# Two decoder layers on one core: the MLP up product of six chunks in eight with the weights as the standing operand

## Chip, cores and metric

One core of one Trainium2 chip runs the whole program in one launch. The metric is the device time of that core in microseconds (us), the median of several executions; less is better. TensorE does the matrix products (a load of the standing 128x128 operand, LDWEIGHTS, and then a matmul that streams the other operand through it), VectorE (DVE) and ScalarE (ACT) do elementwise work and empty the accumulators (PSUM, 8 banks of 512 float32 columns), GpSimd (POOL) does a few small steps, and SyncE (SP) issues the transfers (DMA).

## What is computed

Two layers over 256 tokens of width 1024. Layer 0 mixes tokens by block attention, layer 1 by differential attention; the attention code is not touched, apart from the layout of its operands. After it comes the MLP that the change is about, and each half of a layer is closed by a LayerNorm and scaled and shifted by modulation vectors made from a conditioning vector:

```python
def sq_relu_mlp(h, w_up, w_down):          # w_up 1024x4096, w_down 4096x1024
    return jnp.square(jax.nn.relu(h @ w_up)) @ w_down
...
for i in range(DEPTH):                     # DEPTH = 2
    h = x * (1.0 + scale1) + shift1
    y = moba_attention(...) if i % 2 == 0 else diff_attention(...)
    x = layer_norm(DEEPNORM_ALPHA * x + (1.0 + gate1) * y, ...)
    h = x * (1.0 + scale2) + shift2
    y = sq_relu_mlp(h, mlp_w_up[i], mlp_w_down[i])
    x = layer_norm(DEEPNORM_ALPHA * x + (1.0 + gate2) * y, ...)
```

All is float32. The modulation vectors are `silu(c) @ ada_w + ada_b`, twelve vectors of 1024.

## The kernel before, in words

**Three passes.** A float32 product is made of three matmuls: each operand is split into a rounded part `hi` (type float32r) and the remainder `lo`, and `hi*hi + hi*lo + lo*hi` is summed in PSUM (`mm3`, L165 to L168). A weight arrives by DMA in a raw tile of 128x2048 (three buffers); ACT makes `hi` of a piece of 128x1024 (L129), DVE makes `lo` (L130); there are eight buffers of each. A chunk of 512 columns of `w_up` (`load_cols`) or of 512 rows of `w_down` (`load_rows`) is four such pieces.

**Tokens in two blocks.** The 256 tokens are two blocks of 128, b = 0 and 1. The modulated input of a block is transposed so that the width lies on the partitions, and split: tiles `hTh` and `hTl`, of 128 x 4 x 128, two pairs for each block, four buffers each. These 128x128 slices are the standing operand; the weights stream.

**MLP.** The 4096 inner columns are eight chunks of 512 (`NJ`). Step U (`step_up`) makes the up product of a block and a chunk: 8 slices of the width times 3 passes are 24 matmuls that stream 512 weight columns each into one bank `mm`; ACT applies relu and square (L642, L643) into a tile `nat`, with tokens on the partitions. The down product needs the inner columns on the partitions, so step X (`step_up_T`) transposes the tile by four matmuls against an identity (L650) into a bank `tp`, and ACT and DVE split it into `sTh` and `sTl` (L653, L654). Step D (`step_down`) then runs 24 matmuls of 512 columns (L183): 4 slices, 3 passes, 2 halves of the output. The accumulators of D are two banks `ac` for block 0 and two banks `sc` for block 1, open over all eight chunks.

**Boundaries.** Step B (`boundary`) prepares the vectors of the LayerNorm that closes a half layer: it calls `need`, which traces what is still missing of the gate, scale and shift vectors, and broadcasts the gate (L114, L116). Step C (`close`) does the LayerNorm of a block (L275, L278, L288, ..., L294) and `modulate`, which transposes the result (L307) and fills `hTh` and `hTl` (L311, L314, L315) for the next half layer.

**Modulation vectors as filler.** Each vector is eight rows (`ada_rows`, L214 the DMA of 512 KB, L215 a multiply and sum on DVE) and a closing step, in a queue `filler`. A step `f3` in the program takes three from the queue. The residual of a closed block (L320, L321) is put at the head of the same queue.

**Order.** The string `PROGRAM` lists the steps of each layer; their order in it is the order in which they are traced, and this is the priority by which the framework's scheduler fills each engine's queue, at compile time: where the first in line can't yet run by its model of time, one behind it is taken. Each engine and SP's DMA queue then runs its list strictly in order. The tile framework sets the waits, from the tiles and slices that instructions read and write.

Of the kernel before, what the change touches and what calls it, by code (L numbers as in the profile page):

```python
# [16 lines left out]
F32 = mybir.dt.float32  # L17
# [31 lines left out]
    O11 C10 U00 U01 X00 U10 U11 X01 f1 X10 D00 f1 X11 U02 f2 U12 D10 f1 X02 f1 D01 f1 X12 D11 f3 U03 U13  # L49
    f2 X03 D02 f1 X13 f1 U04 f3 U14 D12 f2 X04 D03 f1 X14 D13 U05 f2 U15 f2 X05 D04 f1 X15 D14 f1 U06 f2  # L50
    U16 f2 X06 D05 f1 X16 D15 f1 U07 f2 U17 f2 X07 D06 X17 f1 D07 f1 B1 C01 D16 D17 C11
# [4 lines left out]
    C10 U00 U01 X00 U10 X01 U11 X10 D00 f1 X11 D10 f1 U02 f3 U12 f2 X02 D01 f1 X12 D11 f1 U03 f2 U13 f2  # L56
    X03 D02 f1 X13 D12 f1 U04 f2 U14 f2 X04 D03 f1 X14 D13 f1 U05 f3 U15 f2 X05 D04 f1 X15 D14 f1 U06 f2
    U16 f2 X06 D05 f2 X16 D15 U07 f2 U17 f2 X07 D06 X17 D07 f1 B1 C01 E C11
# [16 lines left out]
def tile_trunk(ctx: ExitStack, tc: tile.TileContext, x, c, moba_w_in, moba_w_out, diff_w_in, diff_w_out,  # L75
# [60 lines left out]
    def load_cols(w, segs):  # L136
        """[1024, 512] columns, as segments (start, width) -> list of KC (hi, lo) [128, 512] operands."""
# [15 lines left out]
    def load_rows(w, r0):  # L153
        """[512, 1024] row segment -> list of 4 (hi, lo) [128, 1024] operands."""
# [20 lines left out]
    def dense2(dsts, lhs, rows, start, stop):  # L175
        """rows: (hi, lo) of [128, 1024]; dsts: the two column halves."""
# [33 lines left out]
    def ada_rows(l, v, j, dst, tag, bufs):  # L210
        """Chunk j of modulation vector v of layer l as a column: sum_k w[k, n] silu(c)[k] + ada_b[n]."""
# [25 lines left out]
    def affine_cols(l, first, prev):  # L237
        """A = g (1 + scale), B = b (1 + scale) + shift for the LayerNorm `prev` feeding this sub-layer."""
# [11 lines left out]
    def pair_tile(tag, bufs):  # L250
        return (ap_.tile([P, 4, P], F32R, tag=tag + "h", name=tag + "h", bufs=bufs),
                ap_.tile([P, 4, P], F32R, tag=tag + "l", name=tag + "l", bufs=bufs))

    def as_ops(pairs):
        return [(h[:, k, :], l[:, k, :]) for h, l in pairs for k in range(4)]

# [9 lines left out]
    def layer_norm(b, accs, gate, parts=None):  # L266
        """z = alpha x + gate y and its statistics; normalised unless `parts` gives the columns as they come."""
# [32 lines left out]
    def modulate(z, A, B):  # L300
        pairs = []
        for h in range(2):
            hi, lo = pair_tile("hT", 4)
# [12 lines left out]
            pairs.append((hi, lo))  # L316
        return pairs
# [7 lines left out]
    # Head pairs are taken in four groups of two; a group's q and k columns form one product.  # L325
# [39 lines left out]
    def softmax(b, sc, sums, scol_i):  # L365
        """sc: [128, 128 or 256] scores in PSUM -> exp(scale (s - max)), row sums in sums[:, scol_i]."""
# [10 lines left out]
    def probs_T(b, mats):  # L377
        """Transposes of [128, n] tiles; returns per matrix the list of [128 keys, 128 queries] operands."""
# [14 lines left out]
    def scores(b, g):  # L393
        """{(pair, component): [128, 128 (b + 1)] PSUM view}; the two row halves use separate banks."""
# [63 lines left out]
    def attend_finish(kind, b, g, on):  # L458
# [3 lines left out]
        if g % 2 == 0:  # L462
            oT[b, g // 2] = pair_tile("sT", 4)
        hi, lo = (t[:, (g % 2) * 2:(g % 2) * 2 + 2, :] for t in oT[b, g // 2])
# [10 lines left out]
    hT0 = [[pair_tile("hT", 4) for _ in range(2)] for _ in range(2)]  # L475
    # v, then q and k of groups 0 and 1
    kacc = [[psum(t) for t in ("mm", "sc", "ac")] for _ in range(2)]

    def first_operand(j):
        """Modulated operand chunk j of both blocks, and the weight rows that meet it."""  # L480
# [23 lines left out]
        for b in range(2):  # L504
            hi, lo = hT0[b][j // 4]
            act.copy(out=hi[:, j % 4, :], in_=full[:, b * P:(b + 1) * P])
            vec.tensor_tensor(out=lo[:, j % 4, :], in0=full[:, b * P:(b + 1) * P], in1=hi[:, j % 4, :], op=ALU.subtract)
# [4 lines left out]
    def first_products(j, ws):  # L512
        for b in range(2):
            hi, lo = hT0[b][j // 4]
# [90 lines left out]
    def step_v(st, b, g2):  # L605
# [20 lines left out]
    def step_out(st, b, g2):  # L626
# [3 lines left out]
        out_proj(acc, g2, b, rows)  # L630

    def step_close(st, b, i):
        l = st["l"]
        st["x", b] = close(l, i, b, st["oacc" if i == 0 else "dacc", l, b], st["bd"])

    def step_up(st, b, j):
# [3 lines left out]
        dense(ps, as_ops(st["x", b]), w)  # L640
# [5 lines left out]
    def step_up_T(st, b, j):  # L646
# [4 lines left out]
        hi, lo = pair_tile("sT", 4)  # L651
# [84 lines left out]
```

## Time and profile before

| | us |
|---|---|
| median of 3 runs | 662.51 |
| lowest and highest run | 658.27, 663.25 |
| profiled execution, from the first to the last instruction (span) | 663.8 |
| MLP of layer 0, about | 165 to 335 |
| attention of layer 1, about | 360 to 460 |
| MLP of layer 1, about | 480 to 643 |

For the profiled execution the page gives its span and no other time. Times in the profile count from the first instruction. Busy time of PE (matmul) and of PEld (LDWEIGHTS) overlap each other, and a matmul's recorded length is longer than its distance to the next, since matmuls are pipelined: the pace is read from the starts. A row of the view of the groups gives line, engine, operation, result and operand names, shapes and count, then busy time and mean length in ns, and last the idle time before and what ended it.

### The profile page before, as it was taken

To read this page: it belongs to the slowest core of one execution; us is meant where nothing else is said; L and a number is where in the kernel's file an instruction comes from. 1 tells how busy PE (TensorE), PEld (TensorE's weight loads), DVE (VectorE), ACT (ScalarE), POOL (GpSimd) and SP (SyncE) were. 2 spreads that over 40 slices of the span, in tenths; PEclk is the share of its full clock that TensorE was granted. 3 is DMA by queue.
4 is the path that set the end of the run, shared out by engine and by line. 5 is a ranking of instruction groups with operands and counts; after the bars stand their busy time and mean duration, and the time that the engine had idled before them with its cause. 6 is when DMAs were issued, how large, how long until landed. Compare 5 with 4: busy or idle time off the path is not lost. (4 is left out here: it accounts for less than half of the span.)

```text
span 663.8 us, 8530 instructions
## 1 busy us (share of the span) xinstructions
PE 630.3 (95%) x3044; PEld 506.1 (76%) x3044; DVE 484.9 (73%) x855; ACT 365.4 (55%) x651; POOL 22.2 (3%) x37
## 2 busy tenths in 40 slices
PE   4999999999999999999969999989999999999994
PEld 3767878877888888888757887767788888888883
DVE  4798899789968677776689978886974535454446
ACT  3457766457654455555255676765774555354520
POOL 0000000000000000000000010021100000000001
PEclk9999999999999999999979999999999999999998
DMA  8987998876789979888953877661565564636401
GB/s 294 408 313 264 315 315 289 295 239 205 268 258 337 325 252 340 318 292 289 358 195 128 297 252 262 236 222 37 182 228 189 169 210 152 227 129 197 183 1 63
DMA packets 65941, 158.23 MB, mean 238 GB/s; under 512 B 4042, under 2 KB 21099, under 8 KB 65899
## 3 DMA queue, kind: packets, MB, share of 16 engines
q1 hardware_dynamic: 65898, 157.68, 68.0%
q8 instruction: 24, 0.39, 0.2%
q14 instruction: 19, 0.15, 0.1%
HBM read 156.62 MB, written 1.05 MB: 238 GB/s over the span
## 5 line engine op out<-in xcount | busy, mean ns | idle before, releaser
L130 DVE TENSOR_TENSOR lo<-raw,hi 128x1024 fp32r<-128x1024 f32 x196 | 231.2, 1198 | 62.7 <-ACT hi L129 60.5
L129 ACT CAST hi<-raw 128x1024 fp32r<-128x1024 f32 x196 | 200.8, 1037 | 65.4 <-PE sc L183 24.4
L166 PE MATMUL mm<-hi,hTh 128*128 128x512 f32 x416 | 167.4, 403 | 5.1 <-ACT hi L129 2.5
L168 PE MATMUL mm<-hi,hTl 128*128 128x512 f32 x416 | 166.6, 400 | 0.0
L167 PE MATMUL mm<-lo,hTh 128*128 128x512 f32 x416 | 165.8, 399 | 0.1
L215 DVE CUSTOM_DVE_ANT_0 aw<-aw,sbc,tabT 128x1024 f32<-128x1024 f32 x96 | 121.8, 1282 | 43.4 <-DMA aw<-in_ada_w_dram 43.2
L166 PEld LDWEIGHTS mm<-hi,hTh 128*128 128x128 f32 x416 | 78.5, 189 | 24.4 <-ACT hi L129 2.9
L168 PEld LDWEIGHTS mm<-hi,hTl 128*128 128x128 f32 x416 | 78.6, 189 | 18.3 <-DVE hTl L315 0.4
L167 PEld LDWEIGHTS mm<-lo,hTh 128*128 128x128 f32 x416 | 78.6, 189 | 18.1 <-DVE lo L130 0.3
L642 ACT ACTIVATE nat<-mm 128x512 f32<-128x512 f32 x32 | 19.1, 597 | 63.6 <-PE mm L168 63.5
L183 PE MATMUL ac<-hi,sTh 128*128 128x512 f32 x160 | 52.2, 405 | 0.0
L183 PE MATMUL ac<-lo,sTh 128*128 128x512 f32 x160 | 50.8, 395 | 0.0
L183 PE MATMUL ac<-hi,sTl 128*128 128x512 f32 x160 | 50.7, 395 | 0.1
L183 PE MATMUL sc<-hi,sTh 128*128 128x512 f32 x144 | 46.7, 405 | 0.0
L183 PE MATMUL sc<-hi,sTl 128*128 128x512 f32 x144 | 45.5, 396 | 0.0
L183 PE MATMUL sc<-lo,sTh 128*128 128x512 f32 x144 | 45.3, 396 | 0.0
L653 ACT CAST sTh<-tp 128x512 fp32r<-128x512 f32 x32 | 18.7, 584 | 46.2 <-PE tp L650 46.2
L654 DVE TENSOR_TENSOR sTl<-tp,sTh 128x512 fp32r<-128x512 f32 x32 | 22.0, 690 | 24.5 <-ACT sTh L653 24.5
L183 PEld LDWEIGHTS ac<-hi,sTl 128*128 128x128 f32 x160 | 29.8, 188 | 6.7 <-DVE sTl L654 0.5
L183 PEld LDWEIGHTS ac<-lo,sTh 128*128 128x128 f32 x160 | 30.0, 188 | 6.3
L373 ACT ACTIVATE p<-sc,mx 128x128 f32<-128x128 f32 (+1 forms) x64 | 26.6, 421 | 12.1 <-DVE mx L370 10.7
L183 PEld LDWEIGHTS ac<-hi,sTh 128*128 128x128 f32 x160 | 28.7, 189 | 4.8
(137 smaller groups left out, 673.3 us busy)
## 6 DMA issues: line engine op xcount, KB each, us to landing
aw<-in_ada_w_dram SPq DMA_DIRECT2D x96, 512.0 KB, 5.4
raw<-in_mlp_w_up_dram SPq DMA_DIRECT2D x32, 1024.0 KB, 7.1
raw<-in_mlp_w_down_dram SPq DMA_DIRECT2D x32, 1024.0 KB, 5.7
raw<-in_diff_w_in_dram SPq DMA_DIRECT2D x16, 512.0 KB, 4.5
raw<-in_moba_w_in_dram SPq DMA_DIRECT2D x24, 256.0 KB, 5.6
raw<-in_moba_w_in_dram SPq DMA_DIRECT2D x8, 512.0 KB, 5.4
raw<-in_moba_w_out_dram SPq DMA_DIRECT2D x4, 1024.0 KB, 7.9
raw<-in_diff_w_in_dram SPq DMA_DIRECT2D x4, 1024.0 KB
```

Of the source, the lines that this page charges most:

```text
L129: act.copy(out=hi[:, :n], in_=raw_ap)
L130: vec.tensor_tensor(out=lo[:, :n], in0=raw_ap, in1=hi[:, :n], op=ALU.subtract)
L166: pe.matmul(dst, lhsT=xh, rhs=wh, start=start, stop=False)
L167: pe.matmul(dst, lhsT=xh, rhs=wl, start=False, stop=False)
L168: pe.matmul(dst, lhsT=xl, rhs=wh, start=False, stop=stop)
L183: pe.matmul(dsts[h], lhsT=a, rhs=w[:, h * 512:(h + 1) * 512], start=start and k == 0 and i == 0, stop=stop and k == n - 1 and i == 2)
L215: vec.tensor_tensor_reduce(out=aw, in0=aw, in1=sbc, scale=1.0, scalar=adab_cols(l, v)[:, j:j + 1], op0=ALU.mult, op1=ALU.add, accum_out=dst)
L373: act.activation(out=pt[:, :n], in_=sc, func=AF.Exp, bias=mx, scale=-1.0, accum_out=sums[:, scol_i:scol_i + 1])
L642: act.activation(out=r, in_=ps, func=AF.Relu)
L653: act.copy(out=hi, in_=t3)
L654: vec.tensor_tensor(out=lo, in0=t3, in1=hi, op=ALU.subtract)
```

## The change

Chunks 0 and 1 of each layer keep steps U and X. Chunks 2 to 7 get a new step Y that makes the up product of both blocks at once, and has no transposes: a 128x128 slice of the weights stands, and the tokens stream, so that the inner columns come out on the partitions.

For this the input tiles get another layout: one tile `hT` of 128 x 4 x 512 holds, for each slice of the width, `hi` of block 0, `hi` of block 1, `lo` of block 0, `lo` of block 1, of 128 tokens each; two buffers of two such tiles. The tiles `sTh` and `sTl` hold both blocks, 128 x 4 x 256, with two buffers each. For the other products `halves`, `block_ops` and `split_ops` cut the 128x128 slices out again.

```diff
+    def act_tiles():
+        return [ap_.tile([P, 4, 4 * P], F32R, tag="hT", name="hT", bufs=2) for _ in range(2)]
+    def split_tiles():
+        return [ap_.tile([P, 4, 2 * P], F32R, tag="sT" + c_, name="sT" + c_, bufs=2) for c_ in "hl"]
+    def halves(t, b):
+        return t[:, :, b * P:(b + 1) * P], t[:, :, (2 + b) * P:(3 + b) * P]
...
     def step_close(st, b, i):
         l = st["l"]
-        st["x", b] = close(l, i, b, st["oacc" if i == 0 else "dacc", l, b], st["bd"])
+        if b == 0:
+            st["x"] = act_tiles() if st["bd"][0] is not None else None
+        close(l, i, b, st["oacc" if i == 0 else "dacc", l, b], st["bd"], st["x"])
...
+    def step_up_both(st, j):
+        l = st["l"]
+        w = step_load(st, ("wu", l, j), lambda: load_cols(w_up[l], [(j * 512, 512)]))
+        x3 = [t[:, k, :] for t in st["x"] for k in range(4)]
+        hi, lo = step_load(st, ("s", j), split_tiles)
+        for pr, tag in enumerate(("mm", "tp")):
+            pss = [psum(tag) for _ in range(2)]
+            cols_ = [slice((2 * pr + i) * P, (2 * pr + i + 1) * P) for i in range(2)]
+            for k in range(KC):
+                def rounded(first, last):
+                    for ps, c_ in zip(pss, cols_):
+                        pe.matmul(ps, lhsT=w[k][0][:, c_], rhs=x3[k], start=first, stop=last)
+                if k == 0:
+                    rounded(True, False)
+                for ps, c_ in zip(pss, cols_):
+                    pe.matmul(ps[:, 0:S], lhsT=w[k][1][:, c_], rhs=x3[k][:, 0:S], start=False, stop=False)
+                if k > 0:
+                    rounded(False, k == KC - 1)
+            r = ap_.tile([P, 512], F32, tag="nat", name="nat", bufs=3)
+            for i, ps in enumerate(pss):
+                act.copy(out=r[:, i * S:(i + 1) * S], in_=ps[:, S:2 * S])
+                vec.tensor_tensor(out=r[:, i * S:(i + 1) * S], in0=ps[:, 0:S], in1=r[:, i * S:(i + 1) * S], op=ALU.add)
+            act.activation(out=r, in_=r, func=AF.Relu)
+            act.activation(out=r, in_=r, func=AF.Square)
+            r3 = r.rearrange("p (k t) -> p k t", t=S)
+            ks = slice(2 * pr, 2 * pr + 2)
+            act.copy(out=hi[:, ks, :], in_=r3)
+            vec.tensor_tensor(out=lo[:, ks, :], in0=r3, in1=hi[:, ks, :], op=ALU.subtract)
```

So a chunk is taken in two pairs of 128 inner columns, the first pair in the two banks `mm`, the second in the two banks `tp`. The rounded weights stand for 512 streamed columns (`hi` and `lo` of 256 tokens), the remainder of the weights for 256 (`hi` alone). The two halves of a bank are then added while it is emptied.

The steps behind chunk 1, in layer 0 (before, after), and in layer 1 likewise:

```diff
-    ... U02 f2 U12 D10 f1 X02 f1 D01 f1 X12 D11 f3 U03 U13
-    f2 X03 D02 f1 X13 f1 U04 f3 U14 D12 f2 X04 D03 f1 X14 D13 U05 f2 U15 f2 X05 D04 f1 X15 D14 f1 U06 f2
-    U16 f2 X06 D05 f1 X16 D15 f1 U07 f2 U17 f2 X07 D06 X17 f1 D07 f1 B1 C01 D16 D17 C11
+    ... Y2 f4 D10 f1 D01 f1 D11 Y3 f3 D02 f1 D12 Y4 f3 D03 f1
+    D13 Y5 f3 D04 f1 D14 Y6 f3 D05 f1 D15 Y7 f2 D06 D07 B1 C01 D16 D17 C11
```

At the end of a layer, then, the last two steps X and the filler steps that stood between X07 and B1 are gone, and Y7 with its two filler steps stands before D06. The attention's steps and their filler counts are as before.

More of the change, by code (lines that the diff above doesn't have):

```diff
@@ L48 @@
     Q12 T12 f2 F1 f2 P3 S5 F2 Q03 T03 f4 P4 F3 S6 Q13 T13 f4 P5 F4 O00 P6 S7 F5 B0 P7 F6 F7 O01 C00 O10
-    O11 C10 U00 U01 X00 U10 U11 X01 f1 X10 D00 f1 X11 U02 f2 U12 D10 f1 X02 f1 D01 f1 X12 D11 f3 U03 U13
-    f2 X03 D02 f1 X13 f1 U04 f3 U14 D12 f2 X04 D03 f1 X14 D13 U05 f2 U15 f2 X05 D04 f1 X15 D14 f1 U06 f2
-    U16 f2 X06 D05 f1 X16 D15 f1 U07 f2 U17 f2 X07 D06 X17 f1 D07 f1 B1 C01 D16 D17 C11
+    O11 C10 U00 U01 X00 U10 U11 X01 f1 X10 D00 f1 X11 Y2 f4 D10 f1 D01 f1 D11 Y3 f3 D02 f1 D12 Y4 f3 D03 f1
+    D13 Y5 f3 D04 f1 D14 Y6 f3 D05 f1 D15 Y7 f2 D06 D07 B1 C01 D16 D17 C11
     """,
@@ L55 @@
     S4 F3 Q12 T12 f2 S5 Q03 T03 Q13 f2 P4 S6 T13 f1 F4 P6 f1 P5 S7 B0 F5 O00 F6 P7 O01 F7 C00 O10 O11
-    C10 U00 U01 X00 U10 X01 U11 X10 D00 f1 X11 D10 f1 U02 f3 U12 f2 X02 D01 f1 X12 D11 f1 U03 f2 U13 f2
-    X03 D02 f1 X13 D12 f1 U04 f2 U14 f2 X04 D03 f1 X14 D13 f1 U05 f3 U15 f2 X05 D04 f1 X15 D14 f1 U06 f2
-    U16 f2 X06 D05 f2 X16 D15 U07 f2 U17 f2 X07 D06 X17 D07 f1 B1 C01 E C11
+    C10 U00 U01 X00 U10 X01 U11 X10 D00 f1 X11 Y2 f4 D10 f1 D01 f1 D11 Y3 f3 D02 f1 D12 Y4 f3 D03 f1
+    D13 Y5 f3 D04 f1 D14 Y6 f3 D05 f1 D15 Y7 f2 D06 D07 B1 C01 E C11
     """,
@@ L247, in affine_cols, with block_ops, split_ops @@
         return A, B
-    def pair_tile(tag, bufs):
-        return (ap_.tile([P, 4, P], F32R, tag=tag + "h", name=tag + "h", bufs=bufs),
-                ap_.tile([P, 4, P], F32R, tag=tag + "l", name=tag + "l", bufs=bufs))
+    def act_tiles():
[4 more added lines that the diff above has]
+        return t[:, :, b * P:(b + 1) * P], t[:, :, (2 + b) * P:(3 + b) * P]
     def as_ops(pairs):
         return [(h[:, k, :], l[:, k, :]) for h, l in pairs for k in range(4)]
+    def block_ops(tiles, b):
+        return as_ops([halves(t, b) for t in tiles])
+    def split_ops(pair, b):
+        return as_ops([tuple(t[:, :, b * P:(b + 1) * P] for t in pair)])
     def load_bcast(src):
@@ L298, in layer_norm, with modulate @@
         return z
-    def modulate(z, A, B):
-        pairs = []
+    def modulate(b, z, A, B, tiles):
         for h in range(2):
-            hi, lo = pair_tile("hT", 4)
+            hi, lo = halves(tiles[h], b)
             ps = psum("tp")
@@ L461, in attend_finish @@
             pe.transpose(out=tp[:, i * P:(i + 1) * P], in_=on[:, i * P:(i + 1) * P], identity=ident)
-        if g % 2 == 0:
-            oT[b, g // 2] = pair_tile("sT", 4)
-        hi, lo = (t[:, (g % 2) * 2:(g % 2) * 2 + 2, :] for t in oT[b, g // 2])
+        if g // 2 not in oT:
+            oT[g // 2] = split_tiles()
+        hi, lo = (t[:, (g % 2) * 2:(g % 2) * 2 + 2, b * P:(b + 1) * P] for t in oT[g // 2])
         t3 = tp[:, 0:256].rearrange("p (k t) -> p k t", t=P)
@@ L472, in attend_finish @@
                                      op0=ALU.mult, op1=ALU.subtract)
-    hT0 = [[pair_tile("hT", 4) for _ in range(2)] for _ in range(2)]
+    hT0 = act_tiles()
     kacc = [[psum(t) for t in ("mm", "sc", "ac")] for _ in range(2)]
@@ L504, in first_operand @@
         for b in range(2):
-            hi, lo = hT0[b][j // 4]
+            hi, lo = halves(hT0[j // 4], b)
             act.copy(out=hi[:, j % 4, :], in_=full[:, b * P:(b + 1) * P])
@@ L513, in first_products @@
         for b in range(2):
-            hi, lo = hT0[b][j // 4]
+            hi, lo = halves(hT0[j // 4], b)
             for s_ in range(3):
@@ L558, in unit @@
         ps = psum("mm")
-        dense(ps, as_ops(hT), w)
+        dense(ps, hT, w)
         return ps
     def out_proj(dsts, g2, b, rows):
-        dense2(dsts, as_ops([oT[b, g2]]), rows, g2 == 0, g2 == 1)
+        dense2(dsts, split_ops(oT[g2], b), rows, g2 == 0, g2 == 1)
     def boundary(l, i):
@@ L575, in boundary, with close @@
         return A, B, g, gb, bb
-    def close(l, i, b, accs, bd):
+    def close(l, i, b, accs, bd, tiles):
         A, B, gate, gb, bb = bd
@@ L588, in close @@
                 sp.dma_start(out=out[0, b * P:(b + 1) * P, c0:c1], in_=z[:, c0:c1])
-            return None
+            return
         z = layer_norm(b, accs, gate)
-        hT = modulate(z, A, B)
+        modulate(b, z, A, B, tiles)
         filler.appendleft(lambda: residual(b, z, gb, bb))
-        return hT
     def run(program, st):
@@ L639, in step_up @@
         ps = psum("mm")
-        dense(ps, as_ops(st["x", b]), w)
+        dense(ps, block_ops(st["x"], b), w)
         r = ap_.tile([P, 512], F32, tag="nat", name="nat", bufs=3)
@@ L683, in tile_trunk @@
         "B": step_bound, "O": step_out, "C": step_close,
-        "U": step_up, "X": step_up_T, "D": step_down, "E": step_down_last,
+        "U": step_up, "X": step_up_T, "Y": step_up_both, "D": step_down, "E": step_down_last,
         "L": lambda st, l: st.__setitem__("l", l),
     }
-    st = {("x", b): hT0[b] for b in range(2)}
+    st = {"x": hT0}
     run(_schedule(), st)
```

17 lines of the change are left out of this document (9 added, 8 removed).

## The prediction, made before the result was known

> **What bounds the kernel now.** I read the page's first part, then the windows of the stages, then the chain of waits in one MLP chunk.
>
> ```profile
> PE 630.3 (95%) x3044; PEld 506.1 (76%) x3044; DVE 484.9 (73%) x855; ACT 365.4 (55%) x651; POOL 22.2 (3%) x37
> ```
> ```profile
> 165.00:325.00 160.00, 159.93 (x725) 130.40 (x724) 120.42 (x152) 80.29 (x99) 0.00 (x0) 1.00 0.86 299
> 360.00:460.00 100.00, 97.74 (x533) 77.03 (x532) 84.20 (x231) 66.87 (x176) 8.92 (x16) 1.00 0.61 213
> 480.00:643.00 163.00, 163.00 (x741) 133.06 (x740) 81.00 (x74) 84.55 (x104) 0.00 (x0) 1.00 0.50 174
> ```
>
> The window rows give PE, PEld, DVE, ACT, POOL, then granted clock, DMA share and GB/s. In both MLPs, 165 to 325 and 480 to 643, PE has no gap, the clock is full, and DVE has room (75% and 50%). Busy PE means little alone, since recorded matmuls overlap; but the chain confirms it:
>
> ```profile
> 515.93 0.44 PE tp L650 x4
> 516.37 5.50 PE ac L183 x24
> 521.87 0.44 PE tp L650 x4
> 522.30 5.49 PE sc L183 x24
> ...
> 539.00 0.44 PE tp L650 x4
> ```
>
> A chunk takes 539.00 - 515.93 = 23.07 us, all of it PE: two transpose groups of 0.44, two down products of 5.50, and for the 48 up matmuls 539.00 - 527.79 = 11.21 us, or 233 ns each. So what PE saves in chunks 2 to 7 comes off the time one for one, twelve times (six chunks, two layers), as long as nothing else becomes late.
>
> **Part 1: the transposes go.** A chunk loses 2 x 0.44 = 0.88 us of PE; twelve chunks, 10.6 us.
>
> **Part 2: the up matmuls change shape, not volume.** Before, 48 matmuls of 512 columns are 24,576 columns. After, each of 4 column groups and 8 slices has one of 512 and one of 256: 32 + 32 matmuls, again 24,576 columns, but 64 weight loads in place of 48. The question is the pace of a 256-column matmul with a load of its own, which the trace doesn't show. The nearest rows:
>
> ```profile
> 504.57 0.40 PE L166 MATMUL mm<-hi,hTh 128*128 128x512 f32 x1
> 504.80 0.39 PE L167 MATMUL mm<-lo,hTh 128*128 128x512 f32 x1
> 505.03 0.40 PE L168 MATMUL mm<-hi,hTl 128*128 128x512 f32 x1
> ```
> ```profile
> 444.00 1.50 PE L442 MATMUL mm<-v,pT 128*128 128x128 f32 x12
> ```
> ```profile
> L166 PEld LDWEIGHTS mm<-hi,hTh 128*128 128x128 f32 x416 | 78.5, 189 | 24.4 <-ACT hi L129 2.9 <-ACT hTh L506 2.8 <-ACT hTh L314 1.5
> L442 PEld LDWEIGHTS mm<-v,pT 128*128 128x128 f32 x72 | 8.9, 191 | 1.9 <-ACT pT L388 1.3
> L442 PE MATMUL mm<-v,pT 128*128 128x128 f32 x24 | 3.3, 279 | 0.9 <-ACT pT L388 0.9
> ```
>
> Twelve 128-column matmuls with twelve loads start within 1.50 - 0.28 = 1.22 us, 11 distances of 111 ns, though each load is recorded as 191. So loads follow each other every 111 ns, and 111 is the floor. If the time of 512 columns scales, 256 take 233/2 = 117 ns (114 at the 227 to 229 of the down product). The other way is a fixed part. Where the clock was granted at 0.52 (row in part 4), two matmuls of 512 columns took 344.48 - 343.63 us, so 425 ns each, which is about 213 at twice that clock:
>
> ```profile
> 343.63 1.05 PE L183 MATMUL sc<-lo,sTh 128*128 128x512 f32 x2
> 344.48 1.06 PE L183 MATMUL sc<-hi,sTl 128*128 128x512 f32 x2
> ```
>
> If the 20 ns by which 233 exceeds that are fixed for each matmul, 256 columns take 107 + 20 = 127. Bounds: 111 to 127. For the 512-column ones, 227 (down product) to 233 (up product). A chunk's up product is then 32 x 0.227 + 32 x 0.111 = 10.82 at best, 32 x 0.233 + 32 x 0.127 = 11.52 at worst, against 11.21: a gain of 0.39 to a loss of 0.31, over twelve 4.7 to -3.7 us. I take nothing, 32 x (0.233 + 0.117) = 11.20, since both middles lie there.
>
> One rule of the Trainium skill speaks against the change. TensorE: Matmul & The Clock Gate, Part 3, "The mechanism", says that a weight load overlaps matmuls in flight only when it addresses other row groups, and its section "LDWEIGHTS (loading the stationary operand)" gives 128/1.2 = 107 ns for a load. All loads and matmuls here take all rows, so by it the 16 more loads of a chunk would cost 1.7 us, twelve times 20.5, and the sum would be an estimated 672. The trace doesn't agree: 233 ns between matmuls of 213 ns of columns, each with a load recorded as 189, leave no room for one unhidden.
>
> **Part 3: emptying costs ACT and DVE more, hidden.** The nearest rows:
>
> ```profile
> L642 ACT ACTIVATE nat<-mm 128x512 f32<-128x512 f32 x32 | 19.1, 597 | 63.6 <-PE mm L168 63.5
> L643 ACT ACTIVATE nat<-nat 128x512 f32<-128x512 f32 x32 | 20.4, 639 | 0.4
> L653 ACT CAST sTh<-tp 128x512 fp32r<-128x512 f32 x32 | 18.7, 584 | 46.2 <-PE tp L650 46.2
> L388 ACT COPY pT<-tp 128x256 f32<-128x256 f32 x12 | 4.4, 379 | 2.4 <-PE tp L386 2.3
> L654 DVE TENSOR_TENSOR sTl<-tp,sTh 128x512 fp32r<-128x512 f32 x32 | 22.0, 690 | 24.5 <-ACT sTh L653 24.5
> L453 DVE TENSOR_TENSOR on<-mm,sums 128x256 f32<-128x256 f32 x4 | 1.7, 418 | 0.7 <-PE mm L442 0.6
> ```
>
> ACT, a chunk: before 2 x (0.597 + 0.639 + 0.584) = 3.64; after four 256-wide copies and two each of relu, square and cast, 4 x 0.379 + 2 x (3 x 0.639) = 5.35: 1.7 more. DVE: before 2 x 0.690 = 1.38; after 4 x 0.418 + 2 x 0.690 = 3.05: 1.7 more. DVE in layer 0's MLP has 120.42/160 x 23.07 = 17.4 us a chunk; 19.1 in some 22.2 is 86%, still under PE, and ACT is lower. Without that cover it is 1.7 x 12 = 20 us. Latency is covered too: Y(j+1) and two down products stand between a Y and the reuse of its banks, and Y(j+1) between Y(j) and its own D. The tightest place is the layer end: after Y7 only D06 (5.5 us) hides copies, add, relu, square, cast and remainder, 2 x 0.379 + 0.418 + 3 x 0.639 + 0.690 = 3.8 us, with a weight piece of about 1.1 ahead of some hops. I take 0; up to 1 us each.
>
> In Y2 the casts into `sT` wait for D10, the last reader of the buffer. Behind them on ACT stand the weight casts for D10's successors; D10 itself has its weights since D00, so it isn't held, and the other down pieces have D10's 5.5 us. I take 0.
>
> **Part 4: the filler.** Layer 0's MLP had 38 filler steps, after it has 26. Counting through the queue, 32 rows of modulation vectors are traced there before and 24 after (two of them forced by B1); eight move to attention of layer 1, where B0 forces 15 in place of 7. But the scheduler runs rows ahead of the string:
>
> ```profile
> 160.00:335.00 175.00, 51.38 (x80) 1.00 0.86 298
> 345.00:450.00 105.00, 20.32 (x32) 1.00 0.66 228
> ```
>
> These windows of L215 show two instructions for a row: 40 rows in layer 0's MLP, 16 in the attention, none later. So it was eight ahead, and only the eight last, traced in layer 1's MLP, aren't needed by B0. If all eight slip, the attention's DVE gets 8 x 51.38/40 = 10.3 us on 84.2 of 100, not yet full, but in a stage where DVE and PE wait for each other. Bounds 0 to 10.3 us; I take 0, as rows are taken wherever SP and DVE are free.
>
> These rows already cost something at the end of layer 0:
>
> ```profile
> 330.01 1.29 DVE L215 CUSTOM_DVE_ANT_0 aw<-aw,sbc,tabT 128x1024 f32<-128x1024 f32 x1 [3.79 <-DMA aw<-in_ada_w_dram]
> ...
> 331.93 1.28 DVE L215 CUSTOM_DVE_ANT_0 aw<-aw,sbc,tabT 128x1024 f32<-128x1024 f32 x1 [0.62 <-DMA aw<-in_ada_w_dram]
> ...
> 333.14 1.28 DVE L275 TENSOR_TENSOR z<-ac,gate 128x512 f32<-128x512 f32 x2
> ```
> ```profile
> 340.61 1.09 PE L307 MATMUL tp<-cs,z 128*128 128x128 f32 x4 [5.72 <-DVE nm L296]
> ```
> ```profile
> 339.00:346.00 7.00, 5.39 (x17) 4.51 (x18) 4.87 (x7) 4.88 (x11) 0.80 (x2) 0.52 0.73 241
> ```
>
> The closing LayerNorm stands on DVE behind two rows that wait for their DMA; PE idles 5.72 us, and then works at a granted clock of 0.52, which costs about half of 5.4 busy us more: some 8 us in all. With fewer rows due there it may shrink, with B1's forced rows it may stay. Bounds -8 to +5 (one more wait of 3.79 and its row); I take 0.
>
> **Sum.** -10.6 + 0 = -10.6 us. The profiled span, 663.8, lies 0.2% above the median of the runs, 662.5, so the difference carries over: **652.0 us**. Its own range adds -4.7 to +3.7 of part 2 and about 4 either way at boundaries: 644 to 660.
>
> **Rivals.** *The gain is given back by the moved rows.* Eight rows of 1.28 us behind B0 on DVE keep the gate and LayerNorm of layer 1's attention late: +10.3, **662**. For it, DVE's 84%; against it, the running ahead just shown. 14%.
>
> *Weight loads bound the short matmuls (slower).* If a float32r load can't be handed over before its recorded 189 ns, each 256-column matmul takes 189 in place of 117: 32 x 0.072 = 2.3 us a chunk, 27.6 in all, **680**. It decides against the change from 117 + 880/32 = 144 ns on. For it: no short float32r matmul in the trace; against it, the 111 ns of L442 with loads of the same recorded length. 8%.
>
> *Block 1 holds block 0 up (slower).* The blocks now share a tile. If the framework kept whole tiles apart, not slices, U00 would wait for block 1's modulated halves. Now the up products of block 0 run meanwhile:
>
> ```profile
> 467.85 0.40 PE L166 MATMUL mm<-hi,hTh 128*128 128x512 f32 x1
> ...
> 475.86 0.66 PE L307 MATMUL tp<-cs,z 128*128 128x128 f32 x4 [0.38 <-DVE z L294]
> ...
> 480.61 0.60 PE L650 MATMUL tp<-cs,nat 128*128 128x128 f32 x4
> ```
>
> About 11 us at each of three boundaries: 652 + 33 = **685**. Against it: in the kernel's first stage, chunk 0's product starts at 12.24, before the cast of chunk 1 into the same tile,
>
> ```profile
> 12.24 0.79 PE L166 MATMUL mm<-hi,hTh 128*128 128x512 f32 x1 [2.47 <-ACT hi L129]
> ```
> ```profile
> 17.63 0.50 ACT L506 CAST hTh<-full 128x128 fp32r<-128x128 f32 x2
> ```
>
> so slices are told apart, at least contiguous ones. 6%.
>
> *The stall at 334.9 goes too:* 652 - 8 = **644**. 6%, of which half lies below 642.
>
> **From cases to numbers.** Forecast 66%, then 14, 8, 6 and 6. A measurement of this kernel can tell about 1% from no change, 655.9 and 669.1 us. Of the forecast nine tenths lie below 655.9; with the last case that is 0.65 faster, less a little for what I can't see in the scheduler's order: 0.63. No change: the rest of the forecast and most of the first rival, 0.20. Slower: 0.17. The range is 642 to 666: it takes in the forecast, the first rival with its bound, and leaves out the two slower cases and half of the last.
>
> **What would show it.** Right: 12 chunks of about 22.2 us between the down products; 256-column matmuls 111 to 127 ns apart; no L650 past chunk 1; PE without gaps in the MLP. Wrong: a pace above 144; PE waiting for `sT`, `hT` or a bank in a Y; a gap over 5 us before the first U00 or V00 of a half layer; rows of L215 crowded before B0's gate.

## The result and the profile after

| | before | after |
|---|---|---|
| median of the runs on one chip, us | 662.88 (658.27 to 664.78, 4 runs) | 646.18 (644.19 to 648.97, 4 runs) |
| profiled execution: span, us | 663.8 | 642.0 |

The ratio is 0.9746, with a 95% interval from 0.9709 to 0.9784. A second measurement, later and on its own, gave medians of 662.85 and 646.13 us (17 and 6 runs; 16.7 apart again) and a ratio of 0.9773 [0.9722, 0.9824]; this second interval alone doesn't exclude a gain of less than 2%. So the change takes 16.7 us off, where 10.6 had been forecast; 646.2 lies inside the range of 642 to 666.

The first part of the page after the change, and then the windows of the two MLPs and of the attention of layer 1 (PE, PEld, DVE, ACT, POOL, granted clock, DMA share, GB/s):

```profile
PE 615.6 (96%) x3140; PEld 503.5 (78%) x3140; DVE 499.8 (78%) x903; ACT 377.5 (59%) x699; POOL 21.7 (3%) x37
```
```profile
165.00:315.00 150.00, 150.00 (x757) 127.22 (x756) 125.95 (x170) 87.17 (x123) 0.00 (x0) 1.00 0.88 307
480.00:620.00 140.00, 140.00 (x710) 119.07 (x709) 75.75 (x86) 76.80 (x109) 0.00 (x0) 1.00 0.52 179
340.00:440.00 100.00, 98.56 (x536) 76.91 (x535) 87.84 (x234) 68.83 (x184) 8.54 (x17) 1.00 0.73 252
```

PE is still the bound: no gap in these windows of the two MLPs and a full clock, with 96 more loads and 14.7 us less busy time in all. DVE in the MLP of layer 0 rises from 75% to 84% (125.95 of 150) and stays under PE.

One chunk of layer 1 in the chain of waits, to be laid beside the chunk of before:

```profile
522.31 5.49 PE ac L181 x24
527.80 5.44 PE sc L181 x24
533.24 0.47 PE mm L680 x2
533.71 0.47 PE mm L685 x4
...
544.34 5.49 PE ac L181 x24
```

The period is 544.34 - 522.31 = 22.03 us, against 23.07: 1.04 less. The up product of both blocks takes 544.34 - 533.24 = 11.10, against 11.21; the two down products 5.49 + 5.44 = 10.93, against 5.50 + 5.49; the transposes' 0.88 is gone. Twelve such chunks make 12.5 us. Inside the up product, a slice of two long and two short matmuls repeats:

```profile
513.56 0.46 PE mm L680 x2
514.02 0.23 PE mm L685 x2
514.24 0.46 PE mm L680 x2
514.70 0.24 PE mm L685 x2
514.94 0.46 PE mm L680 x2
```

From 513.56 to 514.94 two slices take 1.38 us, 0.69 each: two 512-column matmuls of about 229 ns and two 256-column ones of about 115. The new groups, by shape:

```profile
L680 PE MATMUL mm<-hT,hi 128*128 128x512 f32 x192 | 60.0, 394 | 0.0
L685 PE MATMUL mm<-hT,lo 128*128 128x256 f32 x192 | 36.1, 280 | 0.0
L685 PEld LDWEIGHTS mm<-hT,lo 128*128 128x128 f32 x192 | 34.4, 188 | 7.2
L690 ACT COPY nat<-mm 128x256 f32<-128x256 f32 x24 | 7.8, 376 | 52.3 <-PE mm L680 52.3
L691 DVE TENSOR_TENSOR nat<-mm,nat 128x256 f32<-128x256 f32 x24 | 9.0, 419 | 22.7 <-ACT nat L690 22.7
```

These matmuls, and those of the same lines into `tp`, have no idle time before them (0.0 in the last column), so no matmul of a Y waits for `hT` or a bank. The copy and the add have the lengths that had been taken from other rows (379 and 418).

12.5 us are not 16.7. The second place is the end of layer 0, where before PE had stood idle for 5.72 us. The last matmuls of block 0's last down product, before and after:

```profile
324.48 0.61 PE L183 MATMUL ac<-hi,sTl 128*128 128x512 f32 x2
```
```profile
318.00 0.61 PE L181 MATMUL ac<-hi,sTl 128*128 128x512 f32 x2
```

After the change, on DVE and then PE:

```profile
317.91 1.28 DVE L213 CUSTOM_DVE_ANT_0 aw<-aw,sbc,tabT 128x1024 f32<-128x1024 f32 x1 [3.91 <-DMA aw<-in_ada_w_dram]
...
320.35 1.28 DVE L286 TENSOR_TENSOR z<-ac,gate 128x512 f32<-128x512 f32 x2
```
```profile
327.83 0.63 PE L317 MATMUL tp<-cs,z 128*128 128x128 f32 x4 [0.58 <-DVE nm L307]
```
```profile
327.00:334.00 7.00, 6.42 (x33) 5.18 (x32) 6.87 (x9) 6.58 (x14) 0.10 (x1) 1.00 0.87 278
```

A row still waits there for its transfer (3.91 us), but earlier against the down product. The LayerNorm's first step on `z` (320.35) comes 1.74 us behind the recorded end of that product, 318.61; before, it came 8.05 us behind it (333.14 against 325.09). The LayerNorm itself isn't shorter: from its first step to its first transposes it takes 7.48 us, and 7.47 before. PE is idle for 0.58 us only, and the granted clock stays at 1.00 where it had been 0.52.

### The profile page after: what moved, and what is told of

The parts are those of the page before. It is cut to its first block, busy times and chain, and to the rows that moved or that the text cites. A ratio compares the mean times of both kernels' runs of the same rounds, so it can differ in the third digit from the quotient of the medians.

```text
span 642.0 us, 8775 instructions
## 1 busy us (share of the span) xinstructions
PE 615.6 (96%) x3140; PEld 503.5 (78%) x3140; DVE 499.8 (78%) x903; ACT 377.5 (59%) x699; POOL 21.7 (3%) x37
## 4 chain that ended last, share of the span: by engine, by line
PE 64%; DVE 18%; DMA 9%; issue 3%; ACT 3%; POOL 2%; SPq 0%; DVEq 0%; POOLq 0%; ACTq 0%
PE ac L181 12%; PE sc L181 10%; DMA aw<-in_ada_w_dram 7%; PE mm L680 7%; PE tp L680 6%; DVE lo L128 5%; PE mm L164 5%; PE mm L166 5%; PE mm L165 5%; DVE aw L213 5%; PE mm L685 3%; PE tp L685 3%; PE sc L411 1%; ACT hi L127 1%; DVE z L289 1%
## 5 line engine op out<-in xcount | busy, mean ns | idle before, releaser
L127 ACT CAST hi<-raw 128x1024 fp32r<-128x1024 f32 x196 | 201.0, 1035 | 59.5 <-PE sc L181 43.2
L213 DVE CUSTOM_DVE_ANT_0 aw<-aw,sbc,tabT 128x1024 f32<-128x1024 f32 x96 | 121.9, 1280 | 27.4 <-DMA aw<-in_ada_w_dram 27.2
L164 PE MATMUL mm<-hi,hT 128*128 128x512 f32 x224 | 91.6, 410 | 4.9 <-ACT hi L127 2.3
L166 PE MATMUL mm<-hi,hT 128*128 128x512 f32 x224 | 90.2, 403 | 0.0
L165 PE MATMUL mm<-lo,hT 128*128 128x512 f32 x224 | 89.7, 401 | 0.1
L680 PE MATMUL mm<-hT,hi 128*128 128x512 f32 x192 | 60.0, 394 | 0.0
L680 PE MATMUL tp<-hT,hi 128*128 128x512 f32 x192 | 59.7, 392 | 0.0
L164 PEld LDWEIGHTS mm<-hi,hT 128*128 128x128 f32 x224 | 42.3, 189 | 15.8 <-ACT hT L514 2.8
L166 PEld LDWEIGHTS mm<-hi,hT 128*128 128x128 f32 x224 | 42.4, 189 | 9.8 <-DVE hT L325 0.4
L165 PEld LDWEIGHTS mm<-lo,hT 128*128 128x128 f32 x224 | 42.5, 190 | 9.5 <-DVE lo L128 0.3
L685 PEld LDWEIGHTS mm<-hT,lo 128*128 128x128 f32 x192 | 34.4, 188 | 7.2
L685 PEld LDWEIGHTS tp<-hT,lo 128*128 128x128 f32 x192 | 34.4, 188 | 7.1
L685 PE MATMUL mm<-hT,lo 128*128 128x256 f32 x192 | 36.1, 280 | 0.0
L685 PE MATMUL tp<-hT,lo 128*128 128x256 f32 x192 | 36.0, 279 | 0.0
```

The costliest lines, as they stand in the source:

```text
L127: act.copy(out=hi[:, :n], in_=raw_ap)
L164: pe.matmul(dst, lhsT=xh, rhs=wh, start=start, stop=False)
L165: pe.matmul(dst, lhsT=xh, rhs=wl, start=False, stop=False)
L166: pe.matmul(dst, lhsT=xl, rhs=wh, start=False, stop=stop)
L213: vec.tensor_tensor_reduce(out=aw, in0=aw, in1=sbc, scale=1.0, scalar=adab_cols(l, v)[:, j:j + 1], op0=ALU.mult, op1=ALU.add, accum_out=dst)
L680: pe.matmul(ps, lhsT=w[k][0][:, c_], rhs=x3[k], start=first, stop=last)
```

## The experiments

The theory that they test: of 16.7 us some 12.5 come from the chunks and the rest from the smaller stall at the end of layer 0. The rivals put the rest elsewhere: into the new layout of the tiles, into the count of filler steps, or into more per chunk. Every ratio is against the kernel before on the same chip.

**1. The layout alone.** The kernel before, with the tiles, `halves`, `block_ops` and `split_ops` of the changed one, but with its own steps U and X.

```diff
-        dense(ps, as_ops(hT), w)
+        dense(ps, hT, w)
...
+    def act_tiles():
+        return [ap_.tile([P, 4, 4 * P], F32R, tag="hT", name="hT", bufs=2) for _ in range(2)]
```

> The changed kernel's shared tiles for both blocks, but the step order of before, with U and X for all eight chunks (no step Y). Theory A (the gain is 12 chunks of 1.04 us less PE time plus some 8 us at the end of layer 0, where fewer modulation rows are due): the tiles cost and gain nothing, so 662.9, ratio 0.995 to 1.005, and the idle stretch before the closing LayerNorm's transposes at the end of layer 0 is still about 5.7 us. Rival B (the blocks' halves in one tile hold each other up): above 670. Rival C (the new layout itself brings part of the gain): below 657.

Measured: 661.69 us (10 runs), ratio 1.0034 [1.0004, 1.0065], chunks of 23.07 us as before. The layout gives no gain, and sharing a tile between the blocks costs at most 0.7%, by the interval. One thing came out otherwise than expected: PE was idle for only 1.98 us at the end of layer 0 in this trace, with the string of steps of before.

**2. The new step in layer 1 alone.** Layer 0 keeps its old string of steps.

```diff
-    O11 C10 U00 U01 X00 U10 U11 X01 f1 X10 D00 f1 X11 Y2 f4 D10 f1 D01 f1 D11 Y3 f3 D02 ...
+    O11 C10 U00 U01 X00 U10 U11 X01 f1 X10 D00 f1 X11 U02 f2 U12 D10 f1 X02 f1 D01 f1 X12 D11 ...
```

> Step Y in layer 1 alone; layer 0 has the step order of before. Theory A: six chunks of 1.04 us, and layer 0's end as before, so 662.9 - 6.2 = 656.7, ratio 0.990. If the gain at the end of layer 0 came from something that the new steps of layer 1 or the tiles bring: about 649.

Measured: 655.36 us (9 runs), ratio 0.9907 [0.987, 0.9943]: 5.9 us off the 661.28 of before, for six chunks. That is 1.0 a chunk, as the chain shows. The MLP of layer 1 has no rows of modulation vectors left and no stall, so this is the chunks' gain by itself. By the medians layer 0, with what hangs on it, must then have given 16.7 - 5.9 = 10.8, more than its six chunks.

**3. Fewer filler steps without the new step.** The kernel before, with 26 filler steps in layer 0's MLP in place of 38.

```diff
-    ... X13 f1 U04 f3 U14 D12 f2 X04 ... U07 f2 U17 f2 X07 D06 X17 f1 D07 f1 B1 C01 D16 D17 C11
+    ... X13 U04 f1 U14 f2 D12 X04 ... U07 f1 U17 f1 X07 D06 X17 D07 B1 C01 D16 D17 C11
```

> The kernel of before, with 26 in place of 38 filler steps in layer 0's MLP, spread as in the changed kernel (two after each first up product, one after the next down product, none between X07 and B1 behind D06), nothing else changed. Theory A (the boundary's gain belongs to the filler, not to the product): the idle 5.7 us and the slow clock behind it are gone, 662.9 - 6 to 8 = 655 to 657, ratio 0.988 to 0.991. Rival D (the boundary's gain comes from the order of Y7, D06 and D07 and from the transposes X07 and X17 being gone): no difference, ratio 0.997 to 1.003.

Measured: 660.5 us (10 runs), 0.9985 [0.9956, 1.0014]. The count of filler steps alone does nothing that the times show: the trace has 40 rows in that MLP all the same, since the scheduler takes rows ahead of the string. PE is idle for 3.02 us at the layer end.

**4. The new step with 38 filler steps.** The changed kernel, with the filler steps of layer 0's MLP brought back to 38.

```diff
-    ... Y3 f3 D02 f1 D12 Y4 f3 D03 f1 D13 Y5 f3 ... Y7 f2 D06 D07 B1 C01 D16 D17 C11
+    ... Y3 f5 D02 f1 D12 Y4 f5 D03 f1 D13 Y5 f5 ... Y7 f4 D06 f1 D07 f1 B1 C01 D16 D17 C11
```

> The changed kernel with 38 filler steps in layer 0's MLP again, the last two behind D06 and D07 as before the change. Theory A: the 12.5 us of the chunks stay, the stall at the end of layer 0 comes back: about 650, ratio 0.981, with an idle stretch of several us before the closing LayerNorm's transposes. Rival D: as the changed kernel, 646, ratio 0.975, with an idle stretch under 1 us.

Measured: 649.23 us (4 runs), 0.980 [0.973, 0.987]; 3 us above the changed kernel, but the intervals overlap, so by the times alone it is unclear. The trace is clearer: the stall is back.

```profile
331.39 1.04 PE L312 MATMUL tp<-cs,z 128*128 128x128 f32 x4 [4.40 <-DVE nm L302]
```

**5. Transposes put back into the new step.** Eight transposes of a constant table, whose result nobody reads, are added to each Y.

```diff
+        for _ in range(2):
+            tp = psum("mm")
+            for k in range(4):
+                pe.transpose(out=tp[:, k * P:(k + 1) * P], in_=cs[:, 0:P], identity=ident)
```

> The changed kernel, with eight transposes of a constant put back ahead of each Y, into the two mm banks, read by nobody: PE work alone, as much as the removed steps X. Theory A (PE time comes off one for one): 12 x 0.88 = 10.6 us more, about 657, ratio to before 0.990. If PE weren't the bound in these chunks, or if the gain lay mainly at the boundary: under 650.

Measured: 662.74 us (10 runs), 1.0018 [0.9984, 1.0052]: the whole gain is gone, 16.6 us where the transposes alone are 10.6. The chain shows them, and the period that goes with them:

```profile
517.08 5.44 PE sc L181 x24
522.52 0.87 PE mm L677 x8
...
540.06 5.45 PE sc L181 x24
545.50 0.88 PE mm L677 x8
```

522.52 to 545.50 is 22.98 us, 0.95 more than after the change, 11.4 over twelve. The other 5 lie mostly at the end of layer 0 again:

```profile
336.14 0.94 PE L317 MATMUL tp<-cs,z 128*128 128x128 f32 x4 [4.24 <-DVE nm L307]
```

So a change of the chunk's length, with the same string of steps, brings the stall back. This fits a stall that hangs on where the scheduler puts the rows ahead of the layer end; it doesn't show it yet.

**6. The remainder's matmuls halved again.** In Y, each 256-column matmul becomes two of 128 columns, each with a load of its own.

```diff
-                for ps, c_ in zip(pss, cols_):
-                    pe.matmul(ps[:, 0:S], lhsT=w[k][1][:, c_], rhs=x3[k][:, 0:S], start=False, stop=False)
+                for h in range(2):
+                    for ps, c_ in zip(pss, cols_):
+                        pe.matmul(ps[:, h * P:(h + 1) * P], lhsT=w[k][1][:, c_], rhs=x3[k][:, h * P:(h + 1) * P],
+                                  start=False, stop=False)
```

> The changed kernel, with each 256-column matmul of step Y (remainder of the weights) cut into two of 128 columns, one for each token block, each with a weight load of its own: 32 matmuls of 512 and 64 of 128 columns a chunk. Theory A (loads follow each other every 111 ns at the least, and 256 columns take 117 since they are just above that floor): a 128-column matmul takes 111, the chunk 64 x 0.111 - 32 x 0.117 = 3.4 us longer, twelve times 40 us: about 686. If a load could go at the pace of 128 columns (58 ns): 64 x 0.058 - 32 x 0.117 = 0, about 646. If a float32r load is bound by its recorded 189 ns: 8.4 us a chunk, above 745.

Measured: 722.84 us (2 runs), 1.0905 [1.083, 1.098], far above what was expected. Layer 1 behaves as a floor of some 111 ns a load would have it: from the attention's last LayerNorm on it takes 215.4 us in place of 193.6, 21.8 more or 3.63 a chunk. Its rows, starts of groups of matmuls:

```profile
597.83 0.56 PE L686 MATMUL mm<-hT,lo 128*128 128x128 f32 x4
598.22 0.68 PE L680 MATMUL mm<-hT,hi 128*128 128x512 f32 x2
598.75 0.56 PE L686 MATMUL mm<-hT,lo 128*128 128x128 f32 x4
```

A slice takes 598.75 - 597.83 = 0.92 us in place of 0.69. If the long ones still take 0.46, four short matmuls take 0.46, 115 ns each: as much as one of 256 columns. The MLP of layer 0 got 55 us longer (236.9 in place of 181.4). The same matmuls explain about 22 of them; the other 33 had not been expected. PE is idle there for 20.1 us in place of 2.0, and the mean granted clock is 0.94 in place of 1.00. In one such place the rows of modulation vectors stand on DVE ahead of a remainder that PE needs:

```profile
300.42 1.28 DVE L213 CUSTOM_DVE_ANT_0 aw<-aw,sbc,tabT 128x1024 f32<-128x1024 f32 x1 [1.83 <-DMA aw<-in_ada_w_dram]
302.09 1.28 DVE L213 CUSTOM_DVE_ANT_0 aw<-aw,sbc,tabT 128x1024 f32<-128x1024 f32 x1 [0.38 <-DMA aw<-in_ada_w_dram]
...
303.91 1.22 DVE L128 TENSOR_TENSOR lo<-raw,hi 128x1024 fp32r<-128x1024 f32 x1
305.18 1.00 PE L686 MATMUL mm<-hT,lo 128*128 128x128 f32 x7 [2.87 <-DVE lo L128]
```

PE waits 2.87 us for `lo`, `lo` stands behind two rows on DVE, and these had waited for their transfers. The same mechanism as at the layer end, now in the middle of the chunks. How many of the 33 us it makes up, and why the rows fell so badly there, wasn't tried further.

**7. Rows that can't run ahead.** The changed kernel, with the last rows of layer 1's vectors in other buffers, which the gates and LayerNorm tables hold for long.

```diff
-            return lambda: ada_rows(l, v, j, cl[:, j:j + 1], "aw", 2)
+            late = l == 1 and v not in (SCALE1, SHIFT1)
+            return lambda: ada_rows(l, v, j, cl[:, j:j + 1], *(("bc", 3) if late else ("aw", 2)))
```

> The changed kernel, with the rows of the last four modulation vectors of layer 1 (gate 1, scale 2, shift 2, gate 2) loaded into the three buffers of the boundary vectors (bc) in place of the two of the rows (aw). These buffers are taken by the LayerNorm at the end of layer 0 until it is done with them, so these 32 rows can't be run ahead of it. Theory E (layer 0's end is late by rows that aren't due there, run ahead by the scheduler, on DVE ahead of the LayerNorm's first step while their transfer is under way): the first step follows the last down product of block 0 within about 1 us, no idle stretch of PE there, and 1 to 4 us less at that place; 24 rows must then run in layer 1's attention before B0 in place of 12 to 16, up to 10 us of DVE. If those are hidden: 642 to 645; if the first rival of the prediction is right about DVE there: 650 to 656.

Measured: 666.42 us (10 runs), 1.0061 [1.0039, 1.0082]. Layer 0's MLP is no shorter (180.8 us; 181.4 in the changed kernel), so its remaining stall was already near nothing. But attention and the rest of layer 1 take 7.4 and 14.5 us more:

```profile
469.25 0.16 DVE L245 TENSOR_TENSOR B<-B,col 128x8 f32<-128x8 f32 x1
469.50 1.85 ACT L322 ACTIVATE full<-tp,B,A 128x128 f32<-128x128 f32 x5 [0.40 <-DVE B L245]
471.06 1.12 PE L318 MATMUL tp<-cs,z 128*128 128x128 f32 x4 [14.97 <-ACT full L322]
```

PE waits 14.97 us for the modulated input of block 0, this for the shift vector `B`, and `B` for the rows of modulation vectors, with DVE busy for 19.66 of the 21 us from 455 to 476. It is the mechanism of the prediction's first rival, in a harsher form: 32 rows run behind the end of layer 0 here, in place of 20. It takes back more than the whole gain, where 650 to 656 us had been expected.

**8. Rows fetched through GpSimd's queue.**

```diff
-        sp.dma_start(out=aw, in_=ada_wt[l, r0:r0 + P, :])
+        (pool_e if tag == "aw" and (l, v) not in ((0, SCALE1), (0, SHIFT1)) else sp).dma_start(out=aw, in_=ada_wt[l, r0:r0 + P, :])
```

> The changed kernel, with the transfers of the queued modulation rows issued by GpSimd in place of SyncE, so that they stand behind no weight transfer that waits for its buffer. Theory F (the rows come late at layer 0's end because their issue stands behind weight transfers on SyncE's queue): no wait of a row for its transfer before the LayerNorm at layer 0's end, 2 to 4 us less than the changed kernel, 642 to 644. Theory E without F (the transfer itself is late, at a DMA share of 0.9): as the changed kernel, 644 to 649.

Measured: 704.27 us (4 runs), 1.064 [1.0581, 1.0699]. The waits of this kernel, engine and line waiting, what for, us in total, times, longest:

```profile
POOL aw L212 <- DVE col L213: 237.4, 60, 11.6
...
DVE aw L213 <- DMA aw<-in_ada_w_dram: 67.0, 25, 8.3
```

This is far above what either theory expected. DVE waits 67.0 us for rows, against 27.2 in the changed kernel. The issues, with KB each and the median time to landing, here and then in the changed kernel:

```profile
aw<-in_ada_w_dram POOLq DMA_DIRECT2D x80, 512.0 KB, 4.9
```
```profile
aw<-in_ada_w_dram SPq DMA_DIRECT2D x96, 512.0 KB, 5.8
```

By the medians a transfer from this queue lands no later after its issue, so the issues themselves must come late. The first wait line names what held them: GpSimd waited 60 times for DVE to be done with a buffer `aw`. The rows have two such buffers.

The trace of the kernel before shows the same round trip with SyncE's queue. The two last rows ahead of the LayerNorm are issued at 322.56 and 325.64, directly behind the rows that ended at 322.53 and 325.61 and set their buffers free, and run at 330.01 and 331.93, 7.5 and 6.3 us later. In the changed kernel the rows that run at 317.91 and 319.14 are issued at 312.22 and 314.03, again directly behind the rows that free their buffers (312.19 and 314.00). So these issues didn't stand behind weight transfers, as theory F had it. Whether a third buffer takes the wait away wasn't tried.

**9. Rows never fetched, before and after.** Each row still runs on DVE, but reads a table that is already there.

```diff
-            return lambda: ada_rows(l, v, j, cl[:, j:j + 1], "aw", 2)
+            def run():
+                aw = ap_.tile([P, D], F32, tag="aw", name="aw", bufs=2)
+                vec.tensor_tensor_reduce(out=aw, in0=sbc, in1=sbc, scale=1.0, scalar=adab_cols(l, v)[:, j:j + 1],
+                                         op0=ALU.mult, op1=ALU.add, accum_out=cl[:, j:j + 1])
+            return run
```

> The kernel before, with the 96 rows of modulation vectors that the filler steps take no longer fetched: each still runs its 1.28 us on VectorE, but on a table already there (so the values are others, and the rows' transfers of 0.5 MB each are left out). That takes away every wait of VectorE for a row's transfer and about half of the traffic in the stages that have rows. Theory G: VectorE waiting for rows is what stalls TensorE at the end of layer 0. Then the stall there (5.72 us of idle time before the first closing LayerNorm's transposes, and some 3 us at half clock) shrinks below 1 us and the run takes about 654 (8 off 662). Theory H: the stall is the LayerNorm's own length behind the last down product. Then it stays and the time is 660 to 663.

> The changed kernel with the same rows left unfetched. Its profile had 0.58 us of idle time at that place, so little is left to gain: about 644 to 646 by both theories. What counts is its distance from the kernel before without fetched rows. Theory G: only the chunks differ then, 12 x 1.04 = 12.5 us (11.5 to 13.5). Theory H: the distance stays at the 16 us measured with rows.

Measured: 664.67 us (10 runs), 1.0032 [1.0, 1.0064], and 651.71 us (4 runs), 0.9843 [0.9795, 0.9892]. The two differ by 12.96 us, as theory G says and not by 16; the runs lie between 663.20 and 665.44 and between 650.34 and 652.49, at most 15.1 apart. At the layer end both are now alike; first the kernel before, then the changed one:

```profile
332.75 1.29 DVE L279 TENSOR_TENSOR z<-ac,gate 128x512 f32<-128x512 f32 x2 [5.24 <-ACT gate L116]
```
```profile
340.23 0.63 PE L311 MATMUL tp<-cs,z 128*128 128x128 f32 x4 [0.61 <-DVE nm L300]
```
```profile
333.32 0.63 PE L321 MATMUL tp<-cs,z 128*128 128x128 f32 x4 [0.62 <-DVE nm L311]
```

The scheduler now also puts no row into the last 19 us ahead of the LayerNorm. So the pair takes away the rows' waits and the rows' own 1.28 us at that place together, and doesn't tell which of the two made the stall. The trace of the kernel before does: of the 8.05 us by which the LayerNorm came late, 3.79 and 0.62 are waits for transfers, 2.6 the two rows, and 1.1 remain without them.

The time of the first one, 654, was expected wrongly: the stall goes, but the time doesn't. The scheduler takes more rows in the attention of layer 0 (46 in place of 40), and that stage grows from 146.3 us to 151.7. From 105 to 118 us PE is busy for 9.89 of 13 us there, at a granted clock of 0.74, where the kernel before, in the same stretch of time, has it busy for all 13.00 at 1.00. All of the gain is given back in that stage; the same 151.1 in the changed kernel makes it slower than with fetched rows, and than the 644 to 646 expected.

**10. Both kernels a second time**, each with a new profile.

> The kernel before as it was, a second profile. If the stall at the end of layer 0 belongs to the kernel, it shows again 4 to 6 us of idle time there; if it is a matter of when transfers land, anything from 0.5 to 6.

> The changed kernel as it was, for a second profile and a narrower ratio. If the small stall at the end of layer 0 belongs to the kernel, it shows 0.3 to 1.5 us of idle time there again, and the ratio stays at 0.973 to 0.977. If it was luck, 2 to 6 us, and the ratio moves towards 0.98 (12.5 us).

Measured: 662.61 (1 run) and 646.13 us (6 runs). The first closing LayerNorm's transposes, before and after:

```profile
337.29 1.09 PE L307 MATMUL tp<-cs,z 128*128 128x128 f32 x4 [4.01 <-DVE nm L296]
```
```profile
328.21 0.63 PE L317 MATMUL tp<-cs,z 128*128 128x128 f32 x4 [1.15 <-DVE nm L307]
```

The stall is again large before and again small after. The ratio with this second measurement, 0.9773, lies just beyond the 0.973 to 0.977 expected. The stages of the six traces, cut at the first transposes of the closing LayerNorms, in us:

| | until layer 0's MLP | that MLP | attention of layer 1 | MLP of layer 1 and end |
|---|---|---|---|---|
| before, two profiles | 146.3, 145.9 | 194.3, 191.4 | 122.2, 122.3 | 201.0, 201.0 |
| after, two profiles | 146.4, 146.2 | 181.4, 182.0 | 120.6, 120.5 | 193.6, 193.7 |
| before, rows not fetched | 151.7 | 188.5 | 120.3 | 201.0 |
| after, rows not fetched | 151.1 | 182.2 | 120.3 | 194.7 |

In the last two lines the MLPs differ by 6.3 us each, six chunks of 1.04 and no more. In the first two, layer 0's MLP differs by 9 to 13 and the attention behind it by about 1.7. The last column differs by 7.4 there, about 1 more than six chunks. Most of this is where the cut falls: the first up product starts 5.02 us behind these transposes before (467.85) and 4.16 after (452.55). Counted from that product on, the difference is 6.5, and the attention's is 2.5.

And the stall over all fourteen traces, beside the number of rows between the two closing LayerNorms of layer 0, and beside the time from the recorded end of block 0's last down product to the LayerNorm's first step on `z`:

| kernel | rows | until the first step, us | idle time of PE, us |
|---|---|---|---|
| before, two profiles | 40 | 8.05, 5.40 | 5.72, 4.01 |
| experiment 1 | 40 | 3.37 | 1.98 |
| experiment 2 | 40 | 7.01 | 5.49 |
| experiment 3 | 40 | 6.20 | 3.02 |
| experiment 4 | 38 | 5.56 | 4.40 |
| experiment 5 | 39 | 4.95 | 4.24 |
| experiment 6 | 56 | 1.19 | 0.62 |
| experiment 7 | 24 | 1.10 | 0.62 |
| experiment 8 | 45 | 10.15 | 9.67 |
| experiment 9, before and after | 50, 50 | 1.09, 1.10 | 0.61, 0.62 |
| after, two profiles | 36 | 1.74, 2.32 | 0.58, 1.15 |

The number of rows doesn't decide: 40 rows go with 1.98 to 5.72 us of idle time, and 50 and 56 rows with 0.6. What goes with it is how late the first step comes. Where no row runs in the last 15 us ahead of that step (experiments 6, 7 and 9), it follows the down product by 1.1 to 1.2 us. From the first step to the first transposes it is 7.46 to 7.48 us in all fourteen traces.

## Why the prediction was right, and which terms were mis-sized

**What bounds the kernel, and part 1.** Right. PE in the MLPs set the time, and what it saved came off one for one: 6 chunks of layer 1 alone gave 5.9 us. The transposes' 0.88 a chunk was exact.

**Part 2, the pace.** The mechanism was right and the bounds held; the value was a little too cautious. 32 x (0.233 + 0.117) = 11.20 had been taken, equal to before. Measured were 11.10, since the 512-column matmuls came at 229 and not 233, and the down products took 0.06 less. So the term taken as 0 was 12 x 0.16 = -2 us. The rule of the Trainium skill that had been weighed there (TensorE: Matmul & The Clock Gate, Part 3, "The mechanism": a load overlaps matmuls only if it addresses other row groups) is not borne out here; the same section also lets a load into a background weight buffer run ahead. By the rows above, 64 loads of 188 ns are 12.0 us in an up product that takes 11.10 with its matmuls, so they must run under the matmuls; by the prediction's 213 ns for 512 columns, the columns alone fill 640 of a slice's 690 ns. The rival built on a pace of 189 ns falls with it: 115.

**Part 3.** Right. ACT and DVE do more, 12.1 and 14.9 us over the whole run where twelve chunks of 1.7 are 20, and the matmuls of Y wait for none of it (0.0 idle in L680 and L685).

**Part 4, the rows.** The running ahead was right, but its number changed: 36 rows in layer 0's MLP, 20 in the attention, against 40 and 16 (two instructions a row in these windows of the row's line):

```profile
160.00:330.00 170.00, 46.16 (x72) 1.00 0.86 301
335.00:460.00 125.00, 25.39 (x40) 1.00 0.64 219
```

The four moved rows cost the attention nothing that shows; it got 1.7 us shorter. The mis-sized step is "with fewer rows due there it may shrink, with B1's forced rows it may stay. Bounds -8 to +5; I take 0". It shrank. Medians say 16.7 - 13.0 = 3.7 us; the traces say 2.9 to 5.1 of idle time, by the pairs of profiles, and 1.7 to 2.5 in the attention, whose beginning ran at half clock before. That the stall comes from rows standing on DVE ahead of the LayerNorm, and mostly from their waits, rests on experiment 9, where it vanishes with the fetches, and on the table. The prediction had looked to "fewer rows due there"; the table shows that the count isn't what matters. In the changed kernel the last rows stand earlier: in the first pair of profiles the one that waits longest starts 0.70 us ahead of the end of block 0's last down product, and before it started 4.92 us behind it. Why the scheduler placed them so is not settled. Neither the string with 26 filler steps alone (experiment 3) nor Y with 38 filler steps (experiment 4) or with longer chunks (experiment 5) does it.

**The half clock** stood in the prediction as some 2.7 us of that stall's price of 8. Before, the window behind 5.72 us of idle time had a granted clock of 0.52; after, behind 0.58 us, 1.00. This agrees with the Trainium skill's page TensorE: Matmul & The Clock Gate, Part 1, "What's actually happening", by which the clock halves after an idle window of about 3.4 us.

**The rivals.** The one that ends at 644, "the stall goes too", describes best what happened, and it had got 6%; forecast and rival share the chunk's term, so the range held. Its 8 us were too many: they were read from one profile, with the largest stall of that kernel, and by the medians it gave 3.7. That 646.2 lies so near to 644 is in part luck, since the chunks gave 2 us more than this rival had them give. The first rival, rows giving the gain back, did not happen, but experiment 7 shows that such a thing can. That block 1 holds block 0 up is refuted by experiment 1.

## What to carry to other kernels

When the bound engine has no gaps, price a change in one period by the distances of starts in the chain, multiply, and look then at the stage ends on their own: here they gave over a fifth of the gain. An instruction that waits for a transfer in an in-order queue is a stall for everything behind it, so filler work with transfers shouldn't stand just ahead of a LayerNorm that all wait for, nor ahead of casts that feed the matmuls. And where a scheduler fills gaps, taking a wait away may only move work: check the stages before it too.

## What the runs showed of the hardware that was not expected

Matmuls of 256 columns, each with a load of its own, take 115 ns each, and with 128 columns still 115 (experiment 6, by subtraction), near the 111 that the prediction read from L442. So halving the streamed width further only doubled the count. The short matmul of the changed kernel stands about where its columns and the floor of its load cost the same.

A long wait is paid twice. Around the 14.97 us of experiment 7 the mean granted clock was 0.52 over 21 us, in which PE worked for 5.76 us; the four transposes behind the wait took 1.12 us, against 0.63 in the changed kernel:

```profile
455.00:476.00 21.00, 5.76 (x21) 4.21 (x20) 19.66 (x31) 7.63 (x19) 1.72 (x2) 0.52 0.86 288
```
